# Second block's attention scores: two heads at a time on their own rows of the array, a bank for each head, no zero padding

## The chip, the core and the metric

The program runs on one core of one Trainium2 chip. The metric is the time of one execution on the device, in microseconds (us). Before the change three runs gave 1437.74, 1437.94 and 1439.73 us, median 1437.94. A profile records one execution; its rows give start times from the span's start.

## What is computed

The program is a model of two blocks of two layers each, on one sequence of 256 tokens of width 1024. The change concerns the second block's mixing stage, which has two kinds of attention:

```python
# differential attention: 6 heads, each with 2 components c of 32 numbers
sc = einsum('bqhcd,bkhcd->bhcqk', q_blk, k) * scale - slope_h * |i - j|
pr = softmax(sc)
attn = pr[:, :, 0] - lam * pr[:, :, 1]        # the two components of a head
o = rmsnorm(attn @ v, g_sub) * (1 - lam_init)
# window attention: 2 key heads of 64 numbers, 3 query heads (groups g) on each
sc = q . k * scale - slope * dist, masked outside the window
pr = exp(sc - m) / (sum(exp(sc - m)) + exp(sink - m)),  m = max(max(sc), sink)
```

The two outputs and a spatial gating branch are joined, multiplied by an output matrix, normed and added to x; a feed-forward part follows. All of it is float32; TensorE takes a float32 product either in a rounded format, with the high and the low half of each operand as operands of their own (tiles `w`, `hh`, `hl`), or, as in the scores, directly.

## The kernel before

The mixing stage of layer l is the function `mix2` (L1769 on). For layer 0 it occupies about 740 to 870 us of the span, for layer 1 about 1060 to 1205 us. Weights stream from HBM; ScalarE rounds each into the high half (L384, L390) and VectorE takes the low half (L385, L391), in a ring of slots `w`. TensorE multiplies the input by them (`mm<-w,b`), 384, 256 or 512 columns an instruction. As parts of the projection finish, small generators (`use_q`, `use_k`, ...) scale them and turn them over on TensorE (`tp<-identr,ro`).

The queries of differential attention land in `qz`, 12 slabs of 128 rows: each component's 32 rows stand among zeros. `qz` (128x3072) and `qc` (128x1536, the same for window attention, 64 of 128 rows filled) are cleared by GpSimd (L1776, L1778), and `transp_z` fills each from PSUM with 4 or 2 copies on ScalarE (L714). The score of a component and of 128 queries (t = 0 or 1) is then one float32 product over all 128 rows against the whole slab of keys, 256 columns, followed by a bf16 product `identb` x `dist` that adds the distances (L1835, L1836). Two of these fill one PSUM bank `sc` of two. VectorE takes the maximum (L1874), ScalarE the exponentials (L1879), VectorE the sums and the difference (L1881 to L1884); TensorE turns P over (`tp<-identr,P`), ScalarE copies it (`PT`, L1849), and `tp<-dv,PT` multiplies by the values. A step for head h issues the transposes of head h-1, the scores of h and the values of h-2. After head 5, `ya_norm` (L1994) squares on ScalarE (L1997), sums, takes a reciprocal root and multiplies twice on VectorE (L1999 to L2003); then `to_mix3` turns the result over (`tp<-identr,b`), and ScalarE and VectorE split it (L406, L407) as an operand of the output product. Window attention (`swa`) follows with three groups.

The order of the work is set in two steps. A class `Flow` keeps a virtual clock: each TensorE instruction adds its reckoned time (four cycles a column at 2400 a microsecond for float32, so 0.427 for 256 columns), each generator says by `yield` after how long it wants to go on, and `ya_norm` is followed by `yield 7.0`; the projection's products fill the clock in between. Then a scheduler fixes the order on each engine when the program is built; on the chip each engine runs its list strictly in that order. At the start of layer 0's stage GpSimd's queue holds, in order, the DMA of `qs` (L1710), the two clearings, DMAs of `lb` (two), `P` and `bs`, and then the DMA of `k_dist` (L1706), from which ScalarE makes the table `dist` (L1708); behind that cast, on ScalarE, stand the last pieces of the input's high half (L1616, L1618).

Of the kernel before, what the change touches and what calls it, by code (L numbers as in the profile page):

```python
# [14 lines left out]
OP = mybir.AluOpType  # L15
# [207 lines left out]
class Build:  # L223
# [1544 lines left out]
    def mix2(self, l, hs, done):  # L1768
# [3 lines left out]
        with ExitStack() as es:  # L1772
            mp = self.mp = self.pool(f"mix2_{l}", es=es, reuse_waits="tile")
            T = lambda shape, name, dt=F32, bufs=1: mp.tile(shape, dt, name=name, bufs=bufs)
            qz = T([128, 12, 256], "qz")
            nc.gpsimd.memset(qz, 0.0)  # L1776
            qc = T([128, 6, 256], "qc")
            nc.gpsimd.memset(qc, 0.0)  # L1778
# [19 lines left out]
            def use_q(t, ps):  # L1798
                o = T([128, 384], "ro", bufs=2)
                nc.vector.scalar_tensor_tensor(o, ps[:, :384], hs[t].r, self.qs[:, 0], op0=OP.mult, op1=OP.mult)  # L1800
                yield 1.0
                self.transp_z(qz[:, :, t * 128:(t + 1) * 128], o, 3, 4)
                yield 1.6
# [12 lines left out]
            def use_qc(t, ps):  # L1816
# [7 lines left out]
                self.transp_z(qc[:, :, t * 128:(t + 1) * 128], o, 3, 2)  # L1824
# [10 lines left out]
            def scores(ps, q, k, which, t):  # L1835
                te.matmul(ps, q, k, start=True, stop=False)  # L1836
                te.matmul(ps, self.identb, self.dist[:, which, t], start=False, stop=True)

            def diff():
                P, PT = {}, {}  # L1840
                for s in range(8):
# [8 lines left out]
                    if s < 6:  # L1850
                        for t in range(2):
                            diff_scores(s, t, P)
                            yield 0.0
# [14 lines left out]
            def diff_scores(h, t, P):  # L1868
                sl = slopes[6 + h]
                ps = self.sc([128, 2, 256])  # L1870
                for c in range(2):
                    scores(ps[:, c], qz[:, 2 * h + c, t * 128:(t + 1) * 128], kT[:, h // 2, :], 0, t)
                nm = self.small([128, 2], name="nm")
                nc.vector.tensor_reduce(nm, ps, AX.X, OP.max, negate=True)  # L1874
                nc.vector.tensor_scalar(nm, nm, sl, None, op0=OP.mult)
                p = P[h, t] = T([128, 2, 256], "P", bufs=2)
                sm = self.small([128, 2], name="sums")
                for c in range(2):
                    nc.scalar.activation(p[:, c], ps[:, c], AF.Exp, bias=nm[:, c:c + 1], scale=sl,  # L1879
                                         accum_out=sm[:, c:c + 1])  # L1880
                nc.vector.reciprocal(sm, sm)  # L1881
                nc.vector.tensor_tensor(sm[:, 1:2], sm[:, 1:2], self.nlam[:, l:l + 1], OP.mult)
                nc.vector.tensor_scalar(p[:, 0], p[:, 0], sm[:, 0:1], None, op0=OP.mult)
                nc.vector.scalar_tensor_tensor(p[:, 0], p[:, 1], sm[:, 1:2], p[:, 0], op0=OP.mult, op1=OP.add)  # L1884

            def swa(ready):
# [3 lines left out]
                for s in range(5):  # L1890
# [9 lines left out]
                    if s < 3:  # L1900
                        for t in range(2):
                            swa_scores(s, t, P)
                            yield 0.0
# [12 lines left out]
            def swa_scores(g, t, P):  # L1916
                ps = self.sc([128, 2, 256])
                for kv in range(2):
                    scores(ps[:, kv], qc[:, 2 * g + kv, t * 128:(t + 1) * 128], kc[:, 0, :], 1, t)
                nm = self.small([128, 2], name="nm")  # L1920
                nc.vector.tensor_reduce(nm, ps, AX.X, OP.max)
                for kv in range(2):
                    nc.vector.tensor_scalar(nm[:, kv:kv + 1], nm[:, kv:kv + 1], slopes[3 * kv + g], None, op0=OP.mult)
                sk = self.sink[:, l, g:6:3]
                nc.vector.tensor_tensor(nm, nm, sk, OP.max)
                es_ = self.small([128, 2], name="esink")
                nc.vector.tensor_tensor(es_, sk, nm, OP.subtract)
                nc.vector.tensor_scalar(nm, nm, -1.0, None, op0=OP.mult)
                p = P[g, t] = T([128, 2, 256], "P", bufs=2)
                sm = self.small([128, 2], name="sums")  # L1930
                for kv in range(2):
                    nc.scalar.activation(p[:, kv], ps[:, kv], AF.Exp, bias=nm[:, kv:kv + 1], scale=slopes[3 * kv + g],
# [233 lines left out]
```

## Time and profile before

| | |
|---|---|
| median of three runs | 1437.94 us (1437.74 to 1439.73) |
| the profiled execution | 1439.67 us, span 1437.9 us |
| TensorE busy | 1352.6 us, 94% of the span; granted clock 0.97 on the mean |
| VectorE busy | 874.6 us (61%) |
| ScalarE busy | 671.2 us (47%) |
| GpSimd busy | 77.7 us (5%) |
| chain that ended last | TensorE 46%, VectorE 5%, DMA 4%, ScalarE 2% of the span |

Rows of the trace name an instruction by line, engine, operation, and output<-inputs with buffer numbers left out; "128*64" behind a TensorE operation is the part of the array (rows*columns) that it uses. A float32 product of 256 columns shows as two records (passes). Ends of TensorE's records are modelled and overlap the next start, so its pace is read from start to start. Averages over the span hide the stages: what counts here is read from the two windows of the mixing stage.

### The profile page before, as it was taken

How to read it: one execution, taken by the hardware profiler on the slowest of the kernel's cores; microseconds unless marked ns; L12 is line 12 of the kernel's file. 1: busy time of each engine (PE TensorE's matmuls, PEld its weight loads, DVE VectorE, ACT ScalarE, POOL GpSimd, SP SyncE). 2: the span in 40 equal slices, each digit the busy share in tenths (PEclk: the TensorE clock that was granted, in tenths of full speed). 3: DMA queues.
4: the chain of work that ended last, by engine and by line, in shares of the span. 5: the costliest groups of instructions: out<-in, count | busy, mean ns of one | idle time of the engine just before them, and what ended most of it. 6: DMA issues, size and time to landing. Idle time of an engine off the chain costs nothing.

```text
span 1437.9 us, 18539 instructions
## 1 busy us (share of the span) xinstructions
PE 1352.6 (94%) x6642; PEld 974.2 (68%) x6642; DVE 874.6 (61%) x2094; ACT 671.2 (47%) x1355; POOL 77.7 (5%) x102
## 2 busy tenths in 40 slices
PE   5899998999889999899988998999999998999997
PEld 1667675743375767554448876888878886888885
DVE  1787567222369777522257887555578887655567
ACT  1535334211254543421148756555557856655554
POOL 3210000000011010000020000000010000000000
PEclk9899897899999999999999999999999999999999
DMA  9776587399956656459975343555564533465550
GB/s 344 252 263 214 182 341 290 147 384 413 353 204 235 235 210 240 174 215 411 408 284 205 107 143 117 177 184 195 185 195 149 177 101 132 156 196 186 195 191 29
DMA packets 129590, 317.04 MB, mean 220 GB/s; under 512 B 10164, under 2 KB 67676, under 8 KB 119251
## 3 DMA queue, kind: packets, MB, share of 16 engines
q1 hardware_dynamic: 125538, 304.95, 59.4%
q0 software_dynamic: 3952, 10.83, 2.6%
q8 instruction: 54, 0.88, 0.2%
q14 instruction: 46, 0.37, 0.1%
HBM read 312.59 MB, written 3.16 MB: 220 GB/s over the span
## 4 chain that ended last, share of the span: by engine, by line
PE 46%; DVE 5%; DMA 4%; ACT 2%; issue 1%; POOL 0%; SPq 0%; DVEq 0%; ACTq 0%
PE sc L89 22%; PE mm L89 17%; PE tp L89 4%; PE tp L93 3%; DVE w L391 2%; DMA wf<-in_w_up_dram 2%; DMA wf<-in_w_down_dram 2%; ACT w L390 1%; DMA b<-in_k_dist_dram 1%; DVE b L1751 0%; DVE b L1759 0%; DVE b L407 0%; ACT junk L1747 0%; ACT qz L714 0%; DVE rs_t L426 0%
## 5 line engine op out<-in xcount | busy, mean ns | idle before, releaser
L89 PE MATMUL mm<-w,b 128*128 128x512 f32 (+3 forms) x1920 | 453.4, 384 | 13.3 <-ACT b L1618 6.0
L89 PEld LDWEIGHTS mm<-w,b 128*128 128x128 f32 x1920 | 343.0, 192 | 76.2 <-ACT b L1618 6.6
L89 PE MATMUL sc<-w,b 128*128 128x512 f32 x1056 | 250.2, 392 | 3.7 <-DVE b L407 3.2
L391 DVE SCALAR_TENSOR_TENSOR w<-wf,vt,w 128x512 fp32r<-128x512 f32 (+2 forms) x304 | 199.8, 705 | 47.5 <-ACT w L390 47.2
L89 PEld LDWEIGHTS sc<-w,b 128*128 128x128 f32 x1056 | 196.0, 188 | 44.8 <-DVE b L407 4.0
L390 ACT ACTIVATE w<-wf,vt 128x512 fp32r<-128x512 f32 (+2 forms) x304 | 188.8, 682 | 46.3 <-PE sc L89 16.6
L385 DVE TENSOR_TENSOR w<-wf,w 128x1024 fp32r<-128x1024 f32 (+1 forms) x140 | 172.0, 1243 | 48.1 <-ACT w L384 46.7
L384 ACT CAST w<-wf 128x1024 fp32r<-128x1024 f32 (+1 forms) x140 | 140.7, 1033 | 83.1 <-DMA wf<-in_w_in_dram 39.0
L89 PE MATMUL tp<-wf,X 128*64 128x512 f32 x512 | 117.5, 596 | 0.0
L89 PE MATMUL mm<-w,fh 128*128 128x512 f32 x352 | 110.5, 395 | 0.0
L89 PEld LDWEIGHTS tp<-wf,X 128*64 128x64 f32 x512 | 38.7, 137 | 66.6 <-issue 63.9
L89 PE MATMUL sc<-wf,d 128*64 128x512 f32 x256 | 68.6, 641 | 11.3 <-DMA wf<-in_w_down_dram 3.8
L89 PEld LDWEIGHTS mm<-w,fh 128*128 128x128 f32 x352 | 64.6, 188 | 12.6
L89 PE MATMUL mm<-w,fl 128*128 128x512 f32 x176 | 68.7, 390 | 0.0
L89 PE MATMUL sc<-wf,cact 128*32 128x512 f32 x384 | 56.6, 699 | 11.4 <-DMA wf<-in_w_ada_dram 7.8
L2043 DVE SCALAR_TENSOR_TENSOR f<-sc,en_r,sl 128x256 f32<-128x256 f32 x44 | 21.2, 482 | 68.4 <-ACT sl L2041 68.4
L406 ACT CAST b<-y 128x512 fp32r<-128x512 f32 x32 | 19.8, 619 | 84.0 <-DVE y L1474 84.0
L89 PEld LDWEIGHTS sc<-wf,d 128*64 128x64 f32 x256 | 22.7, 146 | 52.6 <-issue 37.9
L2041 ACT ACTIVATE sl<-sc,en_r 128x256 f32<-128x256 f32 x44 | 20.4, 464 | 80.6 <-PE sc L89 80.5
L93 PE MATMUL tp<-identr,b 128*128 128x128 f32 (+3 forms) x236 | 38.6, 297 | 18.7 <-DVE b L1759 6.9
L1447 DVE SCALAR_TENSOR_TENSOR hid<-hid,m_gsl,tp 128x256 f32<-128x256 f32 x16 | 7.7, 480 | 78.6 <-ACT hid L1446 78.3
L93 PEld LDWEIGHTS tp<-identr,b 128*128 128x128 f32 (+3 forms) x236 | 29.9, 165 | 33.1 <-issue 11.5
(400 smaller groups left out, 1643.3 us busy)
## 6 DMA issues: line engine op xcount, KB each, us to landing
wf<-in_w_ada_dram SPq DMA_DIRECT2D x48, 1024.0 KB, 6.7
wf<-in_w_ffn_in_dram SPq DMA_DIRECT2D x88, 512.0 KB, 4.8
wf<-in_w_in_dram SPq DMA_DIRECT2D x32, 1024.0 KB, 6.7
wf<-in_w_gate_dram SPq DMA_DIRECT2D x64, 512.0 KB, 9.5
wf<-in_w_up_dram SPq DMA_DIRECT2D x64, 512.0 KB, 10.2
wf<-in_w_down_dram SPq DMA_DIRECT2D x32, 1024.0 KB, 10.2
wf<-in_w_ffn_out_dram SPq DMA_DIRECT2D x22, 1024.0 KB, 4.9
wf<-in_w_out_dram SPq DMA_DIRECT2D x12, 1024.0 KB, 6.4
```

The lines of the kernel that those rows point to most:

```text
L89: return self.behind(self.tc.nc.tensor.matmul(out, lhsT, rhs, **k))
L93: return self.behind(self.tc.nc.tensor.transpose(out, src, ident))
L384: nc.scalar.copy(wh, w)
L385: nc.vector.tensor_tensor(wl, w, wh, OP.subtract)
L390: nc.scalar.activation(wh[:, k], w[:, k], AF.Copy, scale=g)
L391: nc.vector.scalar_tensor_tensor(wl[:, k], w[:, k], g, wh[:, k], op0=OP.mult, op1=OP.subtract)
L406: self.nc.scalar.copy(h, src)
L1447: nc.vector.scalar_tensor_tensor(hid, hid, gsl[:, q:q + 1], gu[:, 1], op0=OP.mult, op1=OP.mult)
L2041: nc.scalar.activation(sl, gu[:, :256], AF.Silu, scale=r)
L2043: nc.vector.scalar_tensor_tensor(f, gu[:, 256:], r, sl, op0=OP.mult, op1=OP.mult)
```

## The change

`qz` and `qc` lose the zeros: `qd` and `qc` are 128 rows x 3 x 256, filled by one copy after each turning-over, and nothing is cleared. A score product now names a slice of rows: 32 rows of a differential component (rows 0 to 31 and 32 to 63 for even heads, 64 to 95 and 96 to 127 for odd ones), 64 rows of a window head. Each component has a PSUM bank of its own for both query halves. The distances are added first, by one bf16 product of 512 columns for each bank, then the four products follow with the components in turn. The maximum is taken a bank at a time, both halves before the first exponential; the small operations on sums are done once for both halves. Each score product adds 0.22 to the virtual clock in place of 0.427.

```diff
-            qz = T([128, 12, 256], "qz")
-            nc.gpsimd.memset(qz, 0.0)
-            qc = T([128, 6, 256], "qc")
-            nc.gpsimd.memset(qc, 0.0)
+            qd = T([128, 3, 256], "qd")
+            qc = T([128, 3, 256], "qc")
...
-                self.transp_z(qz[:, :, t * 128:(t + 1) * 128], o, 3, 4)
+                self.transp(qd[:, :, t * 128:(t + 1) * 128], o, 3)
...
-                self.transp_z(qc[:, :, t * 128:(t + 1) * 128], o, 3, 2)
+                self.transp(qc[:, :, t * 128:(t + 1) * 128], o, 3)
...
-            def scores(ps, q, k, which, t):
-                te.matmul(ps, q, k, start=True, stop=False)
-                te.matmul(ps, self.identb, self.dist[:, which, t], start=False, stop=True)
+            def scores(q, k, rows, which):
+
+                ps = [self.sc([128, 2, 256]) for _ in range(2)]
+                for p in ps:
+                    te.matmul(p, self.identb, self.dist[:, which], start=True, stop=False)
+                for t in range(2):
+                    for p, r in zip(ps, rows):
+                        te.matmul(p[:, t], q[r, t * 128:(t + 1) * 128], k[r], us=0.22, start=False, stop=t == 1)
+                return ps
...
-                        for t in range(2):
-                            diff_scores(s, t, P)
-                            yield 0.0
+                        diff_scores(s, P)
+                        yield 0.0
...
-            def diff_scores(h, t, P):
+            def diff_scores(h, P):
                 sl = slopes[6 + h]
-                ps = self.sc([128, 2, 256])
+                rows = [slice(64 * (h % 2) + 32 * c, 64 * (h % 2) + 32 * c + 32) for c in range(2)]
+                ps = scores(qd[:, h // 2], kT[:, h // 2], rows, 0)
+                nm = self.small([128, 2, 2], name="nm4")
                 for c in range(2):
-                    scores(ps[:, c], qz[:, 2 * h + c, t * 128:(t + 1) * 128], kT[:, h // 2, :], 0, t)
-                nm = self.small([128, 2], name="nm")
-                nc.vector.tensor_reduce(nm, ps, AX.X, OP.max, negate=True)
+                    nc.vector.tensor_reduce(nm[:, c], ps[c], AX.X, OP.max, negate=True)
                 nc.vector.tensor_scalar(nm, nm, sl, None, op0=OP.mult)
-                p = P[h, t] = T([128, 2, 256], "P", bufs=2)
-                sm = self.small([128, 2], name="sums")
-                for c in range(2):
-                    nc.scalar.activation(p[:, c], ps[:, c], AF.Exp, bias=nm[:, c:c + 1], scale=sl,
-                                         accum_out=sm[:, c:c + 1])
+                sm = self.small([128, 2, 2], name="sums4")
+                for t in range(2):
+                    P[h, t] = T([128, 2, 256], "P", bufs=2)
+                    for c in range(2):
+                        nc.scalar.activation(P[h, t][:, c], ps[c][:, t], AF.Exp, bias=nm[:, c, t:t + 1], scale=sl,
+                                             accum_out=sm[:, c, t:t + 1])
...
-            def swa_scores(g, t, P):
-                ps = self.sc([128, 2, 256])
+            def swa_scores(g, P):
+                ps = scores(qc[:, g], kc[:, 0], [slice(0, 64), slice(64, 128)], 1)
...
```

Window attention's maxima, sinks and sums are joined over the halves in the same way. What the change moves on the engines' lists is shown at three places. In these rows a tile keeps its number where that tells it from another of the same name, and "[waits ...]" names the engines or DMA queues whose semaphores the instruction waits on.

TensorE in layer 0, the scores of differential head 1; first before, `sc<-b_7591,qz` being a score and `P` the finished head 0:

```order
L89 MATMUL mm_8056<-w_7851,b_7472 128x384 x2
L89 MATMUL sc<-b_7591,qz 128x256 [waits DVE_49,Activation_49]
L89 LDWEIGHTS identb
L89 MATMUL sc<-dist,identb 128x256
L89 MATMUL sc<-b_7591,qz 128x256
L89 LDWEIGHTS identb
L89 MATMUL sc<-dist,identb 128x256
L93 MATMUL tp<-identr,P 128x128 [waits DVE_49,PE_49]
L93 MATMUL tp<-identr,P 128x128
L89 MATMUL sc<-b_7591,qz 128x256 [waits Activation_49]
L89 LDWEIGHTS identb
L89 MATMUL sc<-dist,identb 128x256
```

TensorE at the same place now, `sc<-b_7589,qd` being a score on a slice of rows:

```order
L89 MATMUL mm_8066<-w_7843,b_7472 128x384 x2
L89 LDWEIGHTS identb [waits DVE_49]
L89 MATMUL sc<-dist,identb 128x512 [waits Activation_49]
L89 MATMUL sc<-b_7589,qd 128x256
L89 LDWEIGHTS identb [waits DVE_49]
L89 MATMUL sc<-dist,identb 128x512 [waits Activation_49]
L89 MATMUL sc<-b_7589,qd 128x256 x2
L93 MATMUL tp<-identr,P 128x128 [waits DVE_49,PE_49]
L93 MATMUL tp<-identr,P 128x128
L89 MATMUL sc<-b_7589,qd 128x256
L93 MATMUL tp<-identr,P 128x128 [waits DVE_49]
L93 MATMUL tp<-identr,P 128x128
```

Four scores with a distance product each (the last ones follow the rows shown) have become two 512-column products and four products on slices of rows, and the scheduler has set the four apart: one, then two, then one, with a full-array product or transposes of `P` between. Such patterns occur in both layers: the four in a row for head 0 and window group 0; one, two, one (as here) for heads 1, 3, 4, 5 and group 2 in layer 0 and heads 1 to 5 and group 2 in layer 1; one and three for head 2 in layer 0; two and two for group 1. Head 0's two distance products stand earlier, in layer 0 ahead of the projection's products that follow the `dist` cast, in layer 1 at the end of the previous stage.

TensorE in layer 0 between the last values of differential attention and the transposes of its normed result `b_7595`; before, 34 products of 512 columns stood there (here the last of them), with the transposes behind them:

```order
L89 MATMUL mm_8466<-w_8063,b_7472 128x512 x2
L89 MATMUL mm_8466<-w_8063,b_7473 128x512
L89 MATMUL mm_8466<-w_8063,b_7472 128x512 x2
L89 MATMUL mm_8466<-w_8063,b_7473 128x512
L89 MATMUL mm_8466<-w_8113,b_7472 128x512 x2
L89 MATMUL mm_8466<-w_8113,b_7473 128x512
L89 MATMUL mm_8466<-w_8113,b_7472 128x512 x2
L89 MATMUL mm_8466<-w_8113,b_7473 128x512
L93 MATMUL tp<-identr,b_7597 128x128 [waits DVE_49,PE_49]
```

TensorE at the same place now, from window group 0's scores (`sc<-b_7589,qc`) on:

```order
L89 MATMUL mm_8426<-w_8127,b_7473 128x512
L89 MATMUL sc<-b_7589,qc 128x256 [waits Activation_49]
L89 MATMUL sc<-b_7589,qc 128x256 x3
L89 MATMUL mm_8426<-w_8148,b_7472 128x512 x2
L89 MATMUL mm_8426<-w_8148,b_7473 128x512
L89 MATMUL mm_8426<-w_8148,b_7472 128x512 x2
L89 MATMUL mm_8426<-w_8148,b_7473 128x512
L89 MATMUL mm_8426<-w_8197,b_7472 128x512 x2
L89 MATMUL mm_8426<-w_8197,b_7473 128x512
L89 MATMUL mm_8426<-w_8197,b_7472 128x512 x2
L89 MATMUL mm_8426<-w_8197,b_7473 128x512
L93 MATMUL tp<-identr,b_7595 128x128 [waits DVE_49,PE_49]
```

Now 18 products of 512 columns stand in that place, with the scores of window group 0 among them (its distance products just ahead of the first row shown). Layer 1 has the same.

VectorE in layer 0, the norm of the differential result (`yass`, then `rs_*` with 12 columns, then L2003 of before, L2008 now); before, the chain stood by itself:

```order
L432 SCALAR_TENSOR_TENSOR rs_t<-rs_t 128x12 [waits DVE_49]
L433 SCALAR_TENSOR_TENSOR rs_y_8407<-rs_t,rs_z 128x12 [waits DVE_49]
L428 TENSOR_TENSOR rs_t<-rs_y_8407 128x12 [waits DVE_49]
L429 TENSOR_TENSOR rs_t<-rs_t,rs_h 128x12 [waits DVE_49]
L435 SCALAR_TENSOR_TENSOR rs_y<-rs_t,rs_y_8407 128x12 [waits DVE_49]
L2002 TENSOR_TENSOR b_7597<-b_7597,rs_y 128x768 [waits DMASW7_49,DVE_49]
L2003 TENSOR_TENSOR b_7597<-b_7597,gsub 128x768 [waits DVE_49]
L1944 BN_STATS gst<-mm_8392 128x6 [waits Activation_49]
```

VectorE at the same place now, from the fourth small step of the chain on:

```order
L426 SCALAR_TENSOR_TENSOR rs_t<-rs_z,rs_v 128x1 [waits DVE_49]
L429 TENSOR_TENSOR rs_t<-rs_t,rs_v 128x12 [waits DVE_49]
L385 TENSOR_TENSOR w_8473<-wf,w_8473 128x1024 [waits Activation_49]
L432 SCALAR_TENSOR_TENSOR rs_t<-rs_t 128x12 [waits DVE_49]
L432 SCALAR_TENSOR_TENSOR rs_t<-rs_t 128x1
L1925 TENSOR_REDUCE nm_8447<-sc 128x2 [waits PE_49]
L433 SCALAR_TENSOR_TENSOR rs_y_8315<-rs_t,rs_z 128x12 [waits DVE_49]
L433 SCALAR_TENSOR_TENSOR rs_y_8415<-rs_t,rs_z 128x1 [waits DVE_49]
L1926 TENSOR_SCALAR nm_8447<-nm_8447 128x2 [waits DVE_49]
L428 TENSOR_TENSOR rs_t<-rs_y_8315 128x12 [waits DVE_49]
L426 SCALAR_TENSOR_TENSOR rs_t<-rs_y_8415,rs_h 128x1 [waits DVE_49]
L429 TENSOR_TENSOR rs_t<-rs_t,rs_h 128x12 [waits DVE_49]
```

The low half of a weight (L385), the two maxima of window group 0 (L1925) and the gating branch's own reciprocal root (`rs_*` with one column) have come in between. Layer 1 has the same.

GpSimd's list loses the two clearings in each layer and keeps its order; SyncE's list is the same.

## Rows read from the trace of the kernel before

**Rows 1.** Busy time by stretch: PE, PEld, DVE, ACT, POOL (instructions), PEclk, DMA share, GB/s.

```profile
760.00:765.00 5.00, 3.37 (x12) 3.29 (x13) 2.68 (x4) 4.90 (x14) 0.00 (x0) 0.74 0.01 2
820.00:840.00 20.00, 20.00 (x104) 16.07 (x104) 17.59 (x50) 10.54 (x21) 0.00 (x0) 1.00 0.36 111
```

**Rows 2.** The chain of waits, start of layer 0's stage: start, us, what.

```profile
744.69 2.67 POOL qz L1776
747.37 1.32 POOL qc L1778
...
750.93 7.53 DMA b<-in_k_dist_dram
```

**Rows 3.** ScalarE in order of time there: start, us, operation, [idle before <-releaser].

```profile
753.67 1.06 ACT L1695 COPY b<-sc 128x512 f32<-128x512 f32 x2
758.48 1.04 ACT L1708 CAST dist<-b 128x1024 bf16<-128x1024 f32 x1 [3.75 <-DMA b<-in_k_dist_dram]
```

**Rows 4.** TensorE in order of time there.

```profile
755.07 2.33 PE L89 MATMUL mm<-w,b 128*128 128x384 f32 x12
761.63 8.97 PE L89 MATMUL mm<-w,b 128*128 128x384 f32 x41 [4.22 <-ACT b L1618]
...
770.68 8.58 PE L89 MATMUL mm<-w,b 128*128 128x384 f32 x48
```

**Rows 5.** TensorE, scores of head 0, first half.

```profile
784.71 0.59 PE L89 MATMUL sc<-b,qz 128*128 128x256 f32 x2
785.14 0.27 PE L89 MATMUL sc<-dist,identb 128*128 128x256 bf16 x1
...
785.79 0.60 PE L93 MATMUL tp<-identr,P 128*128 128x128 f32 x4
```

**Rows 6.** TensorE, into and out of a 4-row product.

```profile
837.92 3.69 PE L89 MATMUL mm<-w,b 128*128 128x512 f32 x15
841.53 0.69 PE L89 MATMUL tp<-gsel,bs 4*128 4x256 f32 x2
842.16 0.44 PE L93 MATMUL tp<-identr,P 128*128 128x128 f32 x2
```

**Rows 7.** TensorE, products on half the columns.

```profile
862.80 2.00 PE L89 MATMUL tp<-PT,b 128*64 128x256 f32 x16
```

**Rows 8.** TensorE, last values, filler, transposes of the normed result.

```profile
821.14 1.10 PE L89 MATMUL tp<-dv,PT 128*128 128x64 f32 x8
822.06 1.86 PE L89 MATMUL mm<-w,b 128*128 128x512 f32 x7
...
823.79 6.42 PE L89 MATMUL mm<-w,b 128*128 128x512 f32 x27
830.04 0.82 PE L93 MATMUL tp<-identr,b 128*128 128x128 f32 x6
```

**Rows 9.** VectorE, the norm of the differential result, and a weight's low half.

```profile
823.85 0.95 DVE L1999 TENSOR_REDUCE yass<-b 128x12 f32<-128x768 f32 x1 [0.55 <-ACT b L1997]
824.83 0.17 DVE L414 TENSOR_SCALAR rs_v<-yass 128x12 f32<-128x12 f32 x1
...
827.68 0.96 DVE L2003 TENSOR_TENSOR b<-b,gsub 128x768 f32<-128x768 f32 x1
...
830.25 1.23 DVE L385 TENSOR_TENSOR w<-wf,w 128x1024 fp32r<-128x1024 f32 x1
```

**Rows 10.** ScalarE, the split of the normed result.

```profile
831.20 0.85 ACT L406 CAST b<-tp 128x512 fp32r<-128x512 f32 x2
```

**Rows 11.** Groups on tile sc, by form: count, ns min/median/max.

```profile
L1879 ACT ACTIVATE P<-sc,nm x24: 457/476/492, 790.8 to 817.7; 128x256 f32<-128x256 f32 x24
L1921 DVE TENSOR_REDUCE nm<-sc x6: 684/690/692, 835.8 to 857.1; 128x2 f32<-128x512 f32 x6
```

**Rows 12.** Busy time by stretch, in the feed-forward part ahead of the stage.

```profile
721.00:725.00 4.00, 0.99 (x3) 0.19 (x2) 4.00 (x9) 3.28 (x7) 0.00 (x0) 0.98 1.02 422
725.00:730.00 5.00, 4.12 (x10) 1.01 (x10) 0.22 (x1) 0.00 (x0) 0.00 (x0) 0.50 1.00 413
```

More of the change, by code (lines that the diff above doesn't have):

```diff
@@ L1900, in swa @@
                     if s < 3:
-                        for t in range(2):
-                            swa_scores(s, t, P)
-                            yield 0.0
+                        swa_scores(s, P)
+                        yield 0.0
                     if s >= 2:
@@ L1914, in swa @@
                     yield 3.6 if s < 3 else 1.6
-            def swa_scores(g, t, P):
-                ps = self.sc([128, 2, 256])
+            def swa_scores(g, P):
+                ps = scores(qc[:, g], kc[:, 0], [slice(0, 64), slice(64, 128)], 1)
+                nm = self.small([128, 2, 2], name="nm4")
                 for kv in range(2):
[L1919 to L1924, printed above, removed]
+                    nc.vector.tensor_reduce(nm[:, kv], ps[kv], AX.X, OP.max)
+                    nc.vector.tensor_scalar(nm[:, kv], nm[:, kv], slopes[3 * kv + g], None, op0=OP.mult)
+                sk = self.sink[:, l, g:6:3][:, :, None].to_broadcast([128, 2, 2])
                 nc.vector.tensor_tensor(nm, nm, sk, OP.max)
-                es_ = self.small([128, 2], name="esink")
+                es_ = self.small([128, 2, 2], name="esink")
                 nc.vector.tensor_tensor(es_, sk, nm, OP.subtract)
                 nc.vector.tensor_scalar(nm, nm, -1.0, None, op0=OP.mult)
[L1929 to L1932, printed above, removed]
-                                         accum_out=sm[:, kv:kv + 1])
+                sm = self.small([128, 2, 2], name="sums4")
+                for t in range(2):
+                    P[g, t] = T([128, 2, 256], "P", bufs=2)
+                    for kv in range(2):
+                        nc.scalar.activation(P[g, t][:, kv], ps[kv][:, t], AF.Exp, bias=nm[:, kv, t:t + 1],
+                                             scale=slopes[3 * kv + g], accum_out=sm[:, kv, t:t + 1])
                 nc.scalar.activation(es_, es_, AF.Exp)
@@ L1936, in swa_scores @@
                 nc.vector.reciprocal(sm, sm)
-                for kv in range(2):
-                    nc.vector.tensor_scalar(p[:, kv], p[:, kv], sm[:, kv:kv + 1], None, op0=OP.mult)
+                for t in range(2):
+                    for kv in range(2):
+                        nc.vector.tensor_scalar(P[g, t][:, kv], P[g, t][:, kv], sm[:, kv, t:t + 1], None, op0=OP.mult)
             def use_b(t, ps):
```

8 lines of the change are left out of this document (5 added, 3 removed).

## The prediction

> **What bounds the kernel now.** I read the page first (TensorE busy 94% of the span, granted clock 0.97), then busy time by stretch, the chain of waits, and each engine in order of time. In the mixing stage TensorE is the bound: in 820 to 840 us it is busy 20.00 of 20 us, VectorE 17.59, ScalarE 10.54 [rows 1]. So what ScalarE and VectorE save there (fewer copies, joined small operations) is worth nothing by itself; a term counts only where it changes TensorE's work or makes it wait. The one place of layer 0's stage where TensorE stands still is its start: 4.22 us idle before 761.63 [rows 4]. The chain of waits leads through GpSimd's two clearings to the DMA of the distance table that was queued behind them [rows 2]. In layer 1 the table is there already, and nobody waits for the clearings.
>
> **1. Front of layer 0.** The clearings take 2.67 and 1.32 us, 3.99 together [rows 2]. Without them the DMA, with four short ones still ahead of it, starts at 750.93 - 3.99 = 746.94 and with its 7.53 us lands at 754.47. ScalarE is free from 753.67 + 1.06 = 754.73, so the cast moves there from 758.48: 3.75 us earlier [rows 3]. TensorE runs dry at 761.63 - 4.22 = 757.41 [rows 4]; its products would now come at 757.88, and head 0's two distance products fill the rest. So -3.75, and no less than -2.7 if the transfer lands 1 us later among the weight transfers; a loss is excluded, since nothing is put in front of it. Behind the idle time the granted clock was 0.74 in 760 to 765 [rows 1]: 41 products took 8.97 us, 0.219 each, against 0.179 (48 in 8.58) afterwards [rows 4], which is 41 x 0.04 = 1.64 us. Without the idle time this goes, unless VectorE's weights then set the pace; bounds 0 and -1.64, I take half, -0.8. Sum **-4.55**.
>
> **2. Scores on TensorE.** Two passes of a score take 785.14 - 784.71 = 0.43, and half a head with its distances 785.79 - 784.71 = 1.08 [rows 5]. So a head or group costs 2.17 before, and there are nine in each layer. After: two distance products of twice the width, as much array time as before's four, 4 x 0.11 = 0.43 (0.11 is what is left of 1.08 for each after the scores); four scores of 0.43 each, of which neighbours on different rows can overlap; and a price for each turn from the full array to a slice of rows and back.
>
> The overlap: no two products on different rows stand in this trace. The nearest rows are products on halves of the columns: 16 passes of 256 columns in 2.00 us, 0.125 each [rows 7], against 0.43 / 2 = 0.215 for a pass alone [rows 5]. I take a neighbouring pair at 0.43, one score's time, and keep 0.86 as the upper end.
>
> The turn: a 4-row product stands between full-array products [rows 6]. It starts 841.53 - 837.92 = 3.61 after the start of 15 products of 0.231 (27 in 823.79 to 830.04 [rows 8]), that is 0.14 late; its two passes last 0.43 and the next start is 0.63 behind, 0.20 more. Together 0.34 a round trip. The other end is 0.
>
> The Trainium skill, TensorEngine Tiling (Array Packing), Key Properties, has the rule that speaks against this change: going over to another tiling mode, other than going to another tile of the same mode, drains the engine. [Rows 6] agree, with 0.34 a round trip; by the rule the term below is +3.94, and without any drain it would be -10.7.
>
> By the lists a head in a row of four costs 0.43 + 2 x 0.43 + 0.34 = 1.63; "one, two, one" 0.43 + 3 x 0.43 + 3 x 0.34 = 2.74; "one, three" 0.43 + 3 x 0.43 + 2 x 0.34 = 2.40; "two, two" 0.43 + 2 x 0.43 + 2 x 0.34 = 1.97. Layer 0 has 2, 5, 1 and 1 of them, 21.33 us; layer 1 has 2, 6, 0 and 1, 21.67; before 9 x 2.17 = 19.53 in each. Sum **+3.94**. Of 43 round trips, 14.6 us are switches, so the lower end is -10.7; without overlap 24 pairs add 10.3, so the upper end is +14.3. Head 0's distance products run in idle time of TensorE in either layer: 2 x 0.43, **-0.86**; if that idle time is gone, 0.
>
> **3. The norm of the differential result.** Before, from the end of the last values (822.06) it took 1.79 us until VectorE summed (823.85) and 4.79 more to the end of the chain, 828.64 [rows 8, 9]. TensorE had 34 products to do and came to the transposes at 830.04: 1.40 us to spare. After, it has 18 x 0.231 = 4.16, two short transposes 0.22, distances 0.43 and group 0's scores in a row 1.20: it comes 6.01 us after the values. VectorE's chain is longer: 1.79 + 4.79, a weight's low half 1.23 [rows 9], two maxima of 0.69 [rows 11], and a dozen small operations, which partly fall in the gaps between dependent ones (bounds 0 and 12 x 0.2 = 2.4, 0.2 being ten small steps' pitch from 824.83 on; I take 0.6, near the lower, because TensorE waits only for the chain's own): 9.79. So TensorE waits 3.8 us in each layer; 0.6 if nothing but the shorter cover counts, 5.6 with all small ones. Queued behind the waiting transposes are the output product and group 1's scores, and nothing on TensorE can pass. Behind the transposes ScalarE splits the result in 0.85 us for both parts [rows 10]; before, nine products covered that, now the next product needs it: 0.5 a layer (0 to 0.85). Sum 2 x 4.3 = **+8.6**.
>
> Such a wait can cost clock. About 3 us of idle time in 721 to 725 were followed by a granted clock of 0.50 in 725 to 730 [rows 12], the lower of the two levels, 1.2 GHz, and the 4.22 us above cost 1.64. I take half of that for each wait, **+1.6** (0 to 3.3).
>
> **4. Both banks for one head.** A head holds both `sc` banks, so the next head's distance products wait for two maxima, 1.38, a scaling and up to four exponentials of 0.476, 1.90 [rows 11], some 3.5 us behind its last score. The lists put projection products, transposes and values there, about as long. I take 0; the upper end is 3 us over both layers.
>
> **Sum.** -4.55 + 3.94 - 0.86 + 8.6 + 1.6 = +8.73 against the profiled execution's 1439.67, 1448.4. That execution is 1.73 above the median of 1437.94, so by the median **1446.7 us**.
>
> **Rivals.**
> *A turn costs nothing* (the other side). The weights loaded for a slice of rows have the same 128 columns as before, so 0.34 may belong to the 4-row product alone. Then the scores give -10.7; TensorE reaches the norm 0.34 earlier in each layer, +0.7: 8.73 - 14.6 + 0.7 = -5.2, **1432.7**. It decides once a round trip costs less than 0.14 (43 x 0.20 = 8.6). Against it: the 4-row product exists at two places a layer with the same spacing. 18 in 100.
> *Rows don't overlap.* Every pair costs 0.86: +10.3; group 0's scores then cover 0.86 more of each norm wait, -1.7: +17.3, **1455.3**. For it: no pair of rows is in the trace; against it, the column pairs. 12 in 100.
> *The norm isn't late.* If VectorE's extra work falls into gaps or TensorE comes later by waits of part 4, the waits and their clock go: 8.73 - 7.6 - 1.6 = -0.5, **1437.5**. For it: 1.40 us to spare before; against it: the list, in which the low half and both maxima stand inside the chain. 17 in 100.
> That the change doesn't do what it says is excluded by the lists.
>
> TensorE: Matmul & The Clock Gate in the Trainium skill, Part 3 on packing, holds that small products in distinct row groups run at once. No row here shows it for rows; by it the second rival falls, and the sum stays +8.73.
>
> **How the numbers follow.** 0.2% of 1438 is 2.9 us, about what a measurement of this kernel can tell. The forecast has 53 in 100, with its own range of 1441 to 1453, 3 of them under 1440.8. Of the norm rival's 17 I put 4 under 1435.0, 11 within and 2 above. Faster 18 + 4 = 22, same 11 + 3 = 14, slower 50 + 12 + 2 = 64. The range 1433 to 1455 leaves out about half of the first and of the second rival.
>
> **What would show it.** The cast of the distance table near 754.7 and TensorE busy through 757 to 762; scores starting in pairs about 0.01 us apart where they stand side by side; 0.1 to 0.2 us lost at each turn; idle time of 3 to 4 us in front of the transposes of the normed result in both layers, with VectorE as releaser, and a lower granted clock behind it. If the pairs start 0.2 apart, or those transposes don't wait, the forecast is wrong there; if the projection's products between heads are broken by waits for exponentials, part 4 was mis-sized.

## The result: 0.5% slower, and the profile after

The changed kernel takes 1446.68 us (median of 20 runs, 1438.43 to 1454.71), the kernel before 1437.93 (20 runs, 1433.72 to 1441.90): a ratio of 1.0051, 95% interval 1.0038 to 1.0063. The forecast was 1446.7. The profiled execution took 1447.61, its span 1445.8; before these were 1439.67 and 1437.9.

Where the time went is read from stages, because the span's first half varies by several us from one execution to the next (in the traces of this case the wait called A below begins between 714.1 and 723.3 us, and nothing ahead of it was changed in any of them). Four waits of TensorE that every profile has mark them: one of about 3.0 us in the feed-forward part (A), and those ahead of the turned input `b` behind each mixing stage and ahead of layer 1's (B, C, D). They are in TensorE's timeline of the kernel after (start, duration, engine, line, operation, output<-inputs, part of the array, shape, count; idle time before and what ended it):

```profile
725.84 1.17 PE L89 MATMUL sc<-wf,d 128*64 128x512 f32 x2 [3.04 <-ACT w L390]
...
884.47 1.29 PE L93 MATMUL tp<-identr,b 128*128 128x128 f32 x8 [1.66 <-DVE b L1759]
...
1094.35 1.29 PE L93 MATMUL tp<-identr,b 128*128 128x128 f32 x8 [1.22 <-DVE b L1759]
...
1228.40 1.29 PE L93 MATMUL tp<-identr,b 128*128 128x128 f32 x8 [1.65 <-DVE b L1759]
```

The same four in the kernel before:

```profile
724.40 1.53 PE L89 MATMUL sc<-wf,d 128*64 128x512 f32 x2 [3.01 <-ACT w L390]
...
882.49 1.29 PE L93 MATMUL tp<-identr,b 128*128 128x128 f32 x8 [1.66 <-DVE b L1759]
...
1092.06 1.29 PE L93 MATMUL tp<-identr,b 128*128 128x128 f32 x8 [1.24 <-DVE b L1759]
...
1220.91 1.29 PE L93 MATMUL tp<-identr,b 128*128 128x128 f32 x8 [1.64 <-DVE b L1759]
```

A stage runs from where one such wait begins to where the next begins; A to B after is (884.47 - 1.66) - (725.84 - 3.04) = 160.01.

| us | A to B (layer 0's mixing) | B to C | C to D (layer 1's mixing) | D to end |
|---|---|---|---|---|
| before | 159.44 | 209.99 | 128.45 | 218.63 |
| after | 160.01 (+0.57) | 210.31 | 133.63 (+5.18) | 219.08 |

So the two mixing stages lost 5.75 us in this pair of profiles, what lies behind them 0.77, and 1.42 lies ahead of A, where the change touches nothing. Layer 0 lost 4.61 less than layer 1, because it alone has the gain at its front.

**The front.** TensorE's timeline there, and then the cast of the distance table on ScalarE's:

```profile
756.70 2.33 PE L89 MATMUL mm<-w,b 128*128 128x384 f32 x12
758.87 0.39 PE L89 MATMUL sc<-dist,identb 128*128 128x512 bf16 x1
759.41 7.68 PE L89 MATMUL mm<-w,b 128*128 128x384 f32 x41
```

```profile
756.24 1.06 ACT L1708 CAST dist<-b 128x1024 bf16<-128x1024 f32 x1
```

The 4.22 us of idle time before the 41 products [rows 4] are gone, and those products take 766.92 - 759.41 = 7.51 us (766.92 is the next start), 0.183 each, against 770.44 - 761.63 = 8.81 and 0.215 before (770.44 is the next start there). The cast stood at 758.48 [rows 3]; since A lies 1.42 later here, it comes 3.66 us sooner in its stage. Later, at 768.45, TensorE waits 0.34 for VectorE's weights, which had been hidden. From the 12 products to head 0's first score it is 781.76 - 756.70 = 25.06 (head 0's distance products, at 758.87, are in it), against 784.71 - 755.07 = 29.64 before [rows 4, 5]: the front is 4.58 shorter.

**The scores.** TensorE, head 0 (four in a row; eight passes), then head 1 ("one, two, one"):

```profile
781.76 1.13 PE L89 MATMUL sc<-b,qd 32*128 32x256 f32 x8
782.83 0.66 PE L93 MATMUL tp<-identr,P 128*128 128x128 f32 x4
...
789.28 0.38 PE L89 MATMUL sc<-dist,identb 128*128 128x512 bf16 x1 [0.21 <-ACT P L1883]
789.58 0.69 PE L89 MATMUL sc<-b,qd 32*128 32x256 f32 x2
790.21 0.39 PE L89 MATMUL sc<-dist,identb 128*128 128x512 bf16 x1
790.53 0.70 PE L89 MATMUL sc<-b,qd 32*128 32x256 f32 x4
791.21 0.41 PE L93 MATMUL tp<-identr,P 128*128 128x128 f32 x2
791.55 0.69 PE L89 MATMUL sc<-b,qd 32*128 32x256 f32 x2
792.18 0.44 PE L93 MATMUL tp<-identr,P 128*128 128x128 f32 x2
```

A score alone takes 790.21 - 789.58 = 0.63 until the full array goes on, a pair on different rows 791.21 - 790.53 = 0.68, and two pairs 1.07. So a second score beside the first is nearly free, and leaving the rows costs about 0.20, as [rows 6] had it. Head 1 takes 792.18 - 789.28 = 2.90, less two transposes at 0.10, 2.70; the forecast had 2.74, and a head before cost 2.17 [rows 5]. TensorE turns 21 times in layer 0 and 22 in layer 1.

**The norm.** TensorE from the last values, in both layers:

```profile
826.29 1.00 PE L89 MATMUL tp<-dv,PT 128*128 128x64 f32 x8
...
835.80 1.47 PE L93 MATMUL tp<-identr,b 128*128 128x128 f32 x6 [2.42 <-DVE b L2008]
837.52 2.44 PE L89 MATMUL mm<-w,b 128*128 128x512 f32 x6 [0.25 <-ACT b L406]
839.90 0.69 PE L89 MATMUL tp<-gsel,bs 4*128 4x256 f32 x2
...
1179.44 0.84 PE L93 MATMUL tp<-identr,b 128*128 128x128 f32 x6 [2.42 <-DVE b L2008]
1180.74 2.93 PE L89 MATMUL mm<-w,b 128*128 128x512 f32 x6 [0.46 <-ACT b L406]
```

VectorE meanwhile in layer 0:

```profile
828.71 0.95 DVE L2004 TENSOR_REDUCE yass<-b 128x12 f32<-128x768 f32 x1
...
830.47 1.22 DVE L385 TENSOR_TENSOR w<-wf,w 128x1024 fp32r<-128x1024 f32 x1
...
832.87 0.69 DVE L1925 TENSOR_REDUCE nm<-sc 128x2 f32<-128x512 f32 x1
...
834.70 0.95 DVE L2008 TENSOR_TENSOR b<-b,gsub 128x768 f32<-128x768 f32 x1
```

The last values end at 826.29 + 0.84 = 827.13 (0.84: the pitch of eight such products). TensorE has nothing left at 835.80 - 2.42 = 833.38, 6.25 later; VectorE's result is there 8.67 later, because the low half of a weight and two maxima stand inside the chain. Before, the same chain had 1.40 us to spare [rows 8, 9]. Behind the wait the clock is low; busy time by stretch (PE, PEld, DVE, ACT, POOL, granted clock PEclk, DMA share, GB/s):

```profile
835.00:840.00 5.00, 3.95 (x13) 2.90 (x13) 4.81 (x10) 1.99 (x8) 0.00 (x0) 0.66 0.29 103
...
1180.00:1185.00 5.00, 4.54 (x14) 2.86 (x13) 4.70 (x12) 2.90 (x11) 0.00 (x0) 0.66 0.07 17
```

At full clock these stretches would show 1.00, as 840 to 845 does. At 0.66 a stretch of 5 us loses 0.34 x 5 = 1.7 us, in either layer. TensorE's pace agrees: six transposes and six products take 839.90 - 835.80 - 0.25 = 3.85 us in layer 0; at 0.10 each for the transposes (four in 0.41 behind 782.83) and 0.231 for the products [rows 8] they would take 2.0, and some 0.2 more if the modelled end of the last transpose counts. So the low clock costs about 1.7 us a wait (the expectations below take 1.9), in layer 1 too, where the two products on 4 rows are slow as well (0.81 to the next start in place of 0.62).

**A gain that nobody had counted.** At the end of window attention 28 products of the output stood ahead of the last transposes before, and 40 now. First the kernel before, then after:

```profile
864.73 6.64 PE L89 MATMUL mm<-w,b 128*128 128x512 f32 x28
...
875.56 5.27 PE L89 MATMUL sc<-w,b 128*128 128x512 f32 x22 [1.59 <-DVE b L407]
```

```profile
865.13 9.36 PE L89 MATMUL mm<-w,b 128*128 128x512 f32 x40
...
877.53 5.28 PE L89 MATMUL sc<-w,b 128*128 128x512 f32 x22 [0.55 <-DVE b L407]
```

With 0.36 us of waiting before and 0.19 now at the neighbouring instructions, TensorE waits 1.95 before and 0.74 after: 1.2 us less, and as much in layer 1. Between the norm's transposes and window attention's last values stand 53 products of 512 columns in place of 77, so 12 more are left for the end (43 in place of 31), and cover a wait.

### The profile page after: what moved, and what is told of

It is laid out like the page before. It is cut to its first block, busy times and chain, and to the rows that moved or that the text cites. A ratio compares the mean times of both kernels' runs of the same rounds, so it can differ in the third digit from the quotient of the medians.

```text
span 1445.8 us, 18328 instructions
## 1 busy us (share of the span) xinstructions
PE 1362.6 (94%) x6603; PEld 963.6 (67%) x6606; DVE 864.8 (60%) x2016; ACT 661.6 (46%) x1333; POOL 70.0 (5%) x98
## 4 chain that ended last, share of the span: by engine, by line
PE 46%; DVE 6%; DMA 3%; ACT 3%; issue 1%; SPq 0%; DVEq 0%; ACTq 0%
PE sc L89 22%; PE mm L89 18%; PE tp L89 4%; PE tp L93 3%; DVE w L391 2%; DMA wf<-in_w_up_dram 2%; DMA wf<-in_w_down_dram 2%; ACT w L390 1%; DVE b L1751 0%; DVE b L1759 0%; DVE rs_t L426 0%; DVE w L385 0%; DVE b L407 0%; ACT b L1616 0%; ACT junk L1747 0%
## 5 line engine op out<-in xcount | busy, mean ns | idle before, releaser
L89 PE MATMUL mm<-w,b 128*128 128x512 f32 (+3 forms) x1920 | 447.5, 382 | 11.1 <-DVE b L620 4.9
L385 DVE TENSOR_TENSOR w<-wf,w 128x1024 fp32r<-128x1024 f32 (+1 forms) x140 | 171.9, 1243 | 51.9 <-ACT w L384 51.5
## 6 DMA issues: line engine op xcount, KB each, us to landing
wf<-in_w_up_dram SPq DMA_DIRECT2D x64, 512.0 KB, 10.2
wf<-in_w_down_dram SPq DMA_DIRECT2D x32, 1024.0 KB, 10.2
```

Source lines behind the costliest of these rows:

```text
L89: return self.behind(self.tc.nc.tensor.matmul(out, lhsT, rhs, **k))
L385: nc.vector.tensor_tensor(wl, w, wh, OP.subtract)
```

## The experiments

Short names: *turns* is the theory that going between the full array and rows costs time; *norm wait*, that VectorE's chain is late; *both banks*, that a head which holds both `sc` banks sets the pace of the heads. Ratios are against the kernel before, with 95% intervals.

**1. The front alone.** The kernel before, with its two clearings set behind the DMA of the distance table on GpSimd's list.

```diff
-        nc.gpsimd.dma_start(kd, A["k_dist"])
+        self.kd = nc.gpsimd.dma_start(kd, A["k_dist"]).ins.name
...
-            nc.gpsimd.memset(qz, 0.0)
+            self.tc.add_manual_dep(nc.gpsimd.memset(qz, 0.0).ins, self.kd, mybir.DependencyInfo(
+                mybir.DependencyClass.NoSync, mybir.DependencyReason.DATA))
```

> The kernel before, with one edit: GpSimd clears qz and qc behind the DMA of the distance table instead of ahead of it; every list but GpSimd's keeps its order. My theory (the cast of the table waits for a transfer that the clearings hold up): the cast starts about 3.75 us earlier, TensorE's 4.2 us of idle time and the slow clock behind it go, -4.5 to -5.4 us, about 1433 us. Rival (the transfer is hidden, or VectorE's weights set the pace anyway): 1437 to 1438 us and a new wait within 10 us behind.

Measured 1435.16 us against 1439.26, 0.9971 (0.9952 to 0.9989). The stage A to B is 6.27 us shorter, the others within 1.5 of before. TensorE ahead of the place of the 4.22 us, at it, and at head 0's first score:

```profile
745.95 2.33 PE L89 MATMUL mm<-w,b 128*128 128x384 f32 x12
748.66 7.67 PE L89 MATMUL mm<-w,b 128*128 128x384 f32 x41 [0.38 <-ACT b L1618]
...
771.15 0.59 PE L89 MATMUL sc<-b,qz 128*128 128x256 f32 x2
```

Of the 4.22 us a wait of 0.38 for ScalarE is left, and one of 0.35 for VectorE's weights has come up at 757.71. So the clearings in front of the DMA were the cause of the idle time, as the chain of waits said [rows 2]. This part of the change by itself is worth 4.1 us by the medians, and 29.64 - (771.15 - 745.95) = 4.4 by the rows from the 12 products to the first score. The other 1.8 of the stage's 6.27 lie between A and those products, where nothing was changed: behind A's wait, 3.0 us long in both, the granted clock was low for a shorter time in this execution (0.94 in 720 to 725, against 0.54 at the same place, 727 to 732, of the kernel before).

**2. Scores in a row.** The changed kernel with the two distance products and the four scores of a head tied together, the transposes of the previous head behind them: 18 round trips in place of 43.

```diff
+                te.strict, te.last = True, None
                 for p in ps:
                     te.matmul(p, self.identb, self.dist[:, which], start=True, stop=False)
                 for t in range(2):
                     for p, r in zip(ps, rows):
                         te.matmul(p[:, t], q[r, t * 128:(t + 1) * 128], k[r], us=0.22, start=False, stop=t == 1)
+                turn()
+                te.strict = False
```

> The changed kernel, with each head's four scores held in a row and the transposes of the head before behind them, so that there are 18 round trips between the full array and rows in place of 43 and all pairs stand side by side. By the turn theory (0.34 us a round trip, a pair costs one score) the scores cost 18 x 1.63 = 29.3 us in place of 43.0: -13.7. The norm's chain on VectorE now has two low halves of weights in it and TensorE has 15 products ahead of the transposes, so the two norm waits grow from 2.4 to about 4 us each: net about -10, 1437 us. Rival (turns cost nothing, the loss is all in the waits): about 1450 us.

Measured 1448.02, 1.0061 (1.0037 to 1.0084): no gain. The scores did get cheaper; TensorE at head 1, and then at the norm:

```profile
789.68 1.13 PE L89 MATMUL sc<-b,qd 32*128 32x256 f32 x8
790.85 0.74 PE L93 MATMUL tp<-identr,P 128*128 128x128 f32 x4
...
823.25 1.10 PE L89 MATMUL tp<-dv,PT 128*128 128x64 f32 x8
...
833.83 1.51 PE L93 MATMUL tp<-identr,b 128*128 128x128 f32 x6 [4.50 <-DVE b L2019]
```

```profile
835.00:840.00 5.00, 4.54 (x14) 2.60 (x13) 3.79 (x14) 1.94 (x8) 0.00 (x0) 0.50 0.68 206
840.00:850.00 10.00, 10.00 (x44) 7.32 (x44) 5.95 (x27) 3.21 (x11) 0.00 (x0) 0.73 0.01 4
```

The four scores take 790.85 - 789.68 = 1.17 us with one turn. But TensorE is through with its work 5.1 us after the last values (829.33 - 824.19), and VectorE is ready 9.6 after them: the wait is 4.50 in each layer where it was 2.42, and the clock behind it lower for longer (0.50 x 5 + 0.27 x 10 = 5.2 us lost in 835 to 850, against 1.7). The expectation took the scores' saving, 6.9 us a layer, to reach the end; some 5.6 of it, by layer 0's rows, were spent in the norm wait and the clock behind it.

**3. The norm first on VectorE.** The changed kernel, with window attention's maxima, the gating branch's statistics and all low halves but two set behind the norm's last step.

```diff
-            nc.vector.tensor_tensor(wl, w, wh, OP.subtract)
+            made = nc.vector.tensor_tensor(wl, w, wh, OP.subtract)
+            self.cuts += 1
+            if self.cuts > 2:
+                self.after_norm(made)
...
-                    nc.vector.tensor_reduce(nm[:, kv], ps[kv], AX.X, OP.max)
+                    self.after_norm(nc.vector.tensor_reduce(nm[:, kv], ps[kv], AX.X, OP.max))
```

> The changed kernel, with one edit on VectorE's list: the maxima of window attention, the gating branch's statistics and all low halves of weights but the next two stand behind the end of the differential norm. TensorE's list ahead of the norm's transposes is the same. By the norm theory the wait of 2.4 us in each layer shrinks to under 0.6, and with it the slower clock behind it (about 1.9 us a layer): -7 to -9 us, about 1439 us. Rival (TensorE waits there for something else, or VectorE's moved work makes it late elsewhere): 1445 us or more.

Measured 1449.43, 1.0059 (1.0035 to 1.0082), the time that the expectation gave to its rival. TensorE:

```profile
828.44 0.84 PE L93 MATMUL tp<-identr,b 128*128 128x128 f32 x6 [0.42 <-DVE b L2011]
...
837.98 1.04 PE L89 MATMUL sc<-dist,identb 128*128 128x512 bf16 x2 [3.01 <-DVE rs_z L419]
```

The norm wait is gone as expected, so VectorE's order was its cause. A wait of 3.01 has come up 10 us later, in both layers, in front of group 1's distance products. The row names a small VectorE step; the bank that they write is read by group 0's exponentials on ScalarE, the third of which ends at 837.84. These wait for the small steps behind the maxima: the maxima, pushed back, end at 832.26, and the last step that the exponentials need only at 836.42, because three low halves of weights, pushed back as well, stand among them. Both banks belong to one group, so nothing of the next can start.

**4. Both edits.** Experiments 2 and 3 together.

> Both edits, scores in a row and the norm first on VectorE. If the two costs are separate they add up: -13.7 for the scores, and the norm waits fall to about 1 us each without the slower clock, -6: about 1427 us, faster than either kernel. If the waits only move (TensorE short of products while a head holds both banks), 1433 us or more.

Measured 1438.24, 0.9999 (0.9982 to 1.0016). The norm wait is 1.20 in both layers and that of group 1's distance products 3.00 in layer 0. Each edit alone gains nothing; together they take back what the change cost, and no more.

**5. The norm first, the maxima left alone.** Experiment 3 without its last edit.

> The changed kernel with VectorE's list edited as in the run that put the norm first, except that the two maxima of window group 0 stay where they were, inside the chain; low halves and the gating statistics stand behind. The chain gets about 1.5 us shorter, so the norm wait falls from 2.4 to about 1 us; the wait of 3.0 us in front of group 1's distances, which moving the maxima brought, should not be there. If the clock falls only after the longer waits, the 1.9 us behind each go too: -3.3 a layer, 1440 us. If the moved work comes back as another wait: 1444 us or more.

Measured 1443.64, 1.0032 (1.0015 to 1.0050). Norm waits of 1.16 and 1.13, clock 1.00 behind them, no wait of 3 us; but two new ones in each layer, 0.44 for a copy on ScalarE and 1.15 for VectorE's `vn`, the step of the gating branch that reads the projection's bank: its statistics come late now.

**6. Four banks for the heads.** Odd heads use the two banks of the projection's second accumulator; the projection makes do with the first.

```diff
-                ps[t] = self.mm(i=key[2] % 2 if key[0] == "in" else t)
+                ps[t] = self.mm(i=key[2] % 2 if key[0] == "in" else 0 if key[0] == "in2" else t)
...
-                ps = [self.sc([128, 2, 256]) for _ in range(2)]
+                self.turnbank = 1 - self.turnbank if which == 0 else 1
+                ps = [self.sc([128, 2, 256]) if self.turnbank else self.mm([128, 2, 256], i=1) for _ in range(2)]
```

> The changed kernel with four score banks: odd differential heads take the two banks that the projections used for the second half of the tokens, the projections keep the other two. Nothing else is changed in the program. Theory that a head's hold on both banks is the root (heads follow each other every 6.9 us in place of 5.6, use up the projection's products between them and leave too few for the norm): the list now has 24 products and no scores ahead of the norm's transposes and VectorE's chain stands nearly alone, so both norm waits and the slow clock behind them go: -2 x (2.4 + 0.3 + 1.9) = -9, about 1437 us; scores as before the edit. Rival (the norm's chain itself is what is longer): the waits stay, 1445 us or more.

Measured 1450.72, 1.0088 (1.0053 to 1.0124). The norm waits are 0.22 and 0.21: with two more banks they are gone. But there are new waits at the projection, once of 2.48 at the front, 0.5 to 0.7 three times, and 1.74 in layer 1. The rows name VectorE or ScalarE; that the banks are behind them is shown by experiments 9 and 10, where the front has its banks back and none of these waits. And in this execution the clock was low in layer 1 (0.70 in 1135 to 1140, 0.50 in 1140 to 1150, 0.80 in 1150 to 1160), which is 1.5 + 5 + 2 = 8.5 us lost. Busy time by stretch:

```profile
1140.00:1150.00 10.00, 10.00 (x32) 6.46 (x32) 3.37 (x8) 4.39 (x13) 0.00 (x0) 0.50 0.00 0
```

**7. Four banks, scores in a row.** Experiments 2 and 6 together.

> Four score banks and each head's four scores in a row (18 round trips in place of 43). In the trace of the run that held them in a row a head's scores and distances cost 1.85 us against about 2.7. If no wait eats the saving this time: 1437 - 15 x 0.85 = about 1425 us, faster than either kernel. If VectorE and ScalarE now limit the heads: waits of 0.3 to 1 us in front of the heads' transposes, 1431 us or more.

Measured 1436.83, 0.9991 (0.9974 to 1.0008). The norm waits are 0.33, those at the front stay (2.47, 0.97, 0.67, 0.48, and 1.74 in layer 1).

**8. Neighbours on the same rows.** As experiment 2, with the four scores ordered by component, so that the list has two products on the same rows side by side.

```diff
-                for t in range(2):
-                    for p, r in zip(ps, rows):
+                for p, r in zip(ps, rows):
+                    for t in range(2):
```

> The run with scores in a row, but with the order of a head's four products changed so that the two on the same rows follow each other: first row slice both halves, then the second. Only one pair in the middle is on different rows. If neighbours on different rows run at once, the row of eight passes takes 0.43 us longer than the 1.07 of the two-pair order, 1.5 us; if the array does each product by itself whatever its rows, the same 1.07. The total says little, since a wait can take up the difference.

One run: 1440.06 us. TensorE at head 1:

```profile
786.03 1.14 PE L89 MATMUL sc<-b,qd 32*128 32x256 f32 x8
787.20 0.74 PE L93 MATMUL tp<-identr,P 128*128 128x128 f32 x4
```

The expectation missed: the eight passes take 1.17, as in the order by turns (1.17 in experiment 2). Starts that belong together stand 13 ns apart here, 7 ns in the changed kernel. So the order of neighbours within a head made no difference here. That each slice of rows goes through its own products at its own pace fits these starts, since the second slice's first product stands behind two of the first slice on the list and starts 13 ns behind the first; only these two orders were tried.

**9. Four banks from the third projection on.** As experiment 7, but the first two pieces of the projection keep all four banks, which are free at that time.

```diff
-                ps[t] = self.mm(i=key[2] % 2 if key[0] == "in" else t)
+                ps[t] = self.mm(i=key[2] % 2 if key[0] == "in" else 0 if key[0] == "in2" and key[2] > 1 else t)
```

> As the run with four score banks and scores in a row, but the first two projections (queries and keys) keep all four projection banks, and only from the third on do the heads take two. The trace of that run had new waits of 0.97, 2.47, 0.67 and 0.48 us at the front of layer 0 and 1.74 in layer 1, where a projection waits for its bank; these should go: 6.3 us less, minus the 0.6 that the changed kernel has there, about 1431 us, faster than both kernels by 0.4%. If those waits are of the clock or of VectorE and not of the banks, no change against 1436.8.

Measured **1428.57** (1425.43 to 1430.70, 6 runs) against 1436.87, 0.9932 (0.9908 to 0.9956): faster than both kernels. TensorE:

```profile
777.73 1.13 PE L89 MATMUL sc<-b,qd 32*128 32x256 f32 x8
...
805.00 1.13 PE L89 MATMUL mm<-b,qd 32*128 32x256 f32 x8
...
815.00 1.00 PE L89 MATMUL tp<-dv,PT 128*128 128x64 f32 x8
...
822.46 0.85 PE L93 MATMUL tp<-identr,b 128*128 128x128 f32 x6 [0.36 <-DVE rs_v L414]
```

VectorE: the low half of a weight and group 0's first maximum, behind the norm's last step (it starts at 821.36 and takes 0.95):

```profile
822.29 1.22 DVE L385 TENSOR_TENSOR w<-wf,w 128x1024 fp32r<-128x1024 f32 x1
...
824.74 0.68 DVE L1941 TENSOR_REDUCE nm<-sc 128x2 f32<-128x512 f32 x1
```

From head 0's scores to head 5's it takes 805.00 - 777.73 = 27.3 us (34.7 after, 781.76 to 816.42; 28.0 before). TensorE is out of work 6.27 us after the last values (822.10 - 815.83), as in the changed kernel, but VectorE's result is there after 6.63 in place of 8.67: the low half and group 0's maxima now come behind the norm. The stages are 152.50 and 125.63, 7.5 and 8.0 shorter than after; the clock behind the norm is 1.00 in both layers.

**10. The same banks, the scores where the scheduler sets them.**

> The same banks as in the run beside it, but the scores as the scheduler sets them, turned to rows and back about 20 times a layer. Turn theory: slower than the run beside it by the turns, about 10 a layer at 0.34 and a few more scores that stand alone, 8 to 12 us, about 1441 us. Rival (turns cost nothing once no head waits for a bank): within 3 us of the run beside it.

Measured 1433.21, 0.9970 (0.9953 to 0.9986), 4.6 us above experiment 9; by stages 3.05 and 2.03, 5.1 in all. It has 37 round trips against 24 and ten more scores that stand alone, which is five more times 0.43. So 5.1 - 2.15 = 2.9 us fall to 13 turns, 0.23 each, and 0.27 if the 0.5 us is added that experiment 9 waits longer between heads. That is less than was expected, but the turns cost time, near the 0.34 of [rows 6].

## Why the prediction was right, term by term

- **Front, -4.55.** The mechanism held: experiment 1 has it alone. The rows from the 12 products to the first score give -4.58. Of the clock's bound of -1.64, 1.30 came out (0.215 to 0.183 for each of 41 products), less the 0.34 that VectorE's weights now cost, for the 0.8 that was taken.
- **Scores, +3.94.** Right: 2.70 for 2.74, 0.63 for a score alone as assumed (0.43 + 0.20), a pair 0.68, 43 round trips. Head by head, with 0.10 taken off for each transpose as for head 1, both layers come out some 0.9 us below the forecast, head 0's distances (-0.86, as forecast: in layer 0 inside the front, in layer 1 ahead of the stage) included. What the Trainium skill says in TensorEngine Tiling (Array Packing), Key Properties, that a change of mode drains the engine, agrees with these 0.20 us; so does what the Trainium skill says in TensorE: Matmul & The Clock Gate, Part 3 on packing, that products in distinct row groups run at once, with 0.05 us for the second of a pair.
- **Norm wait, +7.6, and split, +1.0.** The place, the releaser and the cause were right; the size was not: 2.42 a layer for 3.8, and 0.25 and 0.46 for the split. TensorE came at 6.25 us, 6.01 by the forecast. The step that was mis-sized is the chain, 8.67 for 9.79. It is 0.2 shorter as far as VectorE's sum (`yass`); from there to its end it takes 834.70 + 0.95 - 828.71 = 6.94, and 4.79 + 1.23 + 2 x 0.69 = 7.40 for the chain and the large steps alone. So the dozen small ones, for which 0.6 was taken, cost nothing: they filled gaps, and part of the large ones did too.
- **Clock, +1.6.** Mis-sized, at the upper end of its bounds: 1.7 a wait, 3.4 in all, where 3.3 was the upper end. The forecast took half of the 1.64 that followed 4.22 us of idle time; what followed 2.42 us cost all of it.
- **The tail, not in the sum.** -1.2 a layer, from the output's products that were left over.
- **Both banks, 0.** As waits between heads right: 0.21 and 0.32 are all there is. But the term was put in the wrong place: projection products fill the gaps between heads (30 of the products of 512 columns stand ahead of the last values, 2 before), the heads stand 6.9 us apart in place of 5.6, and the products are missing at the norm. With banks for two heads (experiments 6, 7, 9, 10) the norm wait is 0.2 to 0.4. Experiment 9 shows that this comes less from more products at the norm than from VectorE's list: group 0's scores come later, half of them behind the norm's transposes, and neither their maxima nor a low half stands in the chain any more.

With scores and distances as forecast and the other sizes as measured the two stages come to -4.58 + 3.94 - 0.86 + 5.55 + 3.4 - 2.4 = +5.05, with the 0.53 of waits between heads 5.6, and 5.75 was measured; with the scores head by head 4.7, so about 1 us may be in no term. That the median is 8.75 above the kernel before and the forecast 8.73 is thus partly luck: norm and clock together are 8.95 for 10.2, the tail was left out, and 3 us of the medians' difference (interval 5.5 to 9.1) are not in the profiled stages. Where they lie is open. The clock behind a wait, which varies (last section), is one candidate: the mean granted clock is 0.968 over the 20 executions after, and 0.972 over 70 of the kernel before in the experiments. That is at most 0.004 x 1440 = 5.8 us, of which the norm waits account for 3.4; it was not tried.

The rivals fell. A turn isn't free (experiments 9 and 10, and each row that shows 0.63 for a lone score); rows do overlap; and the norm is late. Experiment 2 adds what the first rival overlooked: with 25 turns fewer the time stays, since the norm wait and the clock behind it take the gain.

## What to carry to other kernels

Before array time is cut, look at what the freed time runs into: here the saving of experiment 2 ended in front of a chain on VectorE that TensorE's work had covered. Ask what a unit of work holds (here both banks) and whether the next one can start while it is held; the fillers spent on that gap are missing somewhere else. Products on slices of rows pay where they stand together, one turn for many, and a clearing in front of a DMA in the same queue is paid for by whoever waits for that DMA.

## What the hardware showed that was not expected

Equal waits are not followed by equal clocks. In experiment 8 TensorE waited 2.46 us for the norm in both layers; busy time by stretch behind the first and the second:

```profile
830.00:835.00 5.00, 5.00 (x12) 3.01 (x12) 2.73 (x7) 1.59 (x7) 0.00 (x0) 0.50 0.17 33
835.00:840.00 5.00, 5.00 (x22) 3.67 (x22) 2.93 (x9) 0.06 (x1) 0.00 (x0) 0.50 0.52 176
...
1175.00:1180.00 5.00, 5.00 (x29) 3.37 (x30) 4.41 (x13) 1.48 (x7) 0.00 (x0) 1.00 0.18 44
```

The granted clock was at its lower level, 1.2 GHz, for 10 us and more in layer 0 (0.92 still in 840 to 850) and did not fall at all in layer 1; after 2.42 us in the changed kernel it was 0.66 over 5 us in both. In experiment 6 it was 0.50 for 10 us with no idle time above 0.48 us in the 30 us ahead. What decides it was not tried, so a forecast for such a kernel should carry the clock behind a wait of some 2.5 us as a range, here from 0 to some 6 us, and not as a share of the wait.
